# Sinks as a column of the softmax, and fewer small operations in cross-attention, in a two-layer encoder kernel

## The chip, the cores and the metric

The kernel runs on one core of one Trainium2 chip. What counts is the device time of one execution in microseconds (us). Engine names are those of the profile: PE is the matrix engine (TensorE), PEld its weight loads, DVE the vector engine (VectorE), ACT the scalar engine (ScalarE), POOL GpSimd, SP the engine that issues most transfers.

## What is computed

Two layers of a bidirectional encoder on 1024 tokens of width 1024, float32. Each layer has a token mixer and a gated feed-forward part with a short convolution; the mixer of layer 0 is windowed attention, that of layer 1 a gated linear recurrence (HGRN2). Beside either mixer run four heads of cross-attention into 256 memory tokens. The parts that matter here, cut:

```python
def window_gqa_sink(q, k, v, sink):          # 16 heads in 4 groups, blocks of 128 queries, band of 384 keys
    s = einsum('bnqhgd,bnkhd->bnhgqk', qb, kb) * (d ** -0.5)          # d = 64, factor 0.125
    s = where(valid, s, -inf)
    m = maximum(max(s, axis=-1), sk)                                  # sk: one sink per head
    p = exp(s - m)
    p = p / (sum(p, axis=-1) + exp(sk - m))
    o = einsum('bnhgqk,bnkhd->bnqhgd', p, vb)

def memory_cross_attn(xq, mem_kv):           # 4 heads of 128
    s = einsum('bthd,bmhd->bhtm', q, k) * (128 ** -0.5)
    o = einsum('bhtm,bmhd->bthd', softmax(s), v)

# layer: h = h + rmsnorm(mixer(rmsnorm(h))); h = h + rmsnorm(conv_ffn(rmsnorm(h)))
```

## The kernel before

A float32 product is made of three matmuls: each operand is split into a rounded part and a remainder, and `mm3` adds high times high, high times low and low times high. `split(h, l, src)` makes the two parts with a cast on ACT (L88) and a subtraction on DVE (L89); `wunit` does the same for weights that come from memory (L78 on ACT, L79 on DVE or, for some of the first mixer's weights, on POOL). So nearly every matmul has an ACT and a DVE instruction ahead of it.

The program is written as one sequence; a planner puts the instructions of each engine into an order with a simulated timeline of its own, by priority and by when operands are ready there. Each engine then runs its list in order, and waits only where data or a buffer is missing. `tc.high_priority` and `tc.issue_after` steer single instructions. Tiles come from pools with a fixed number of buffers per tag; a new tile waits until the last reader of the buffer is done.

The order of the work: `start` (0 to some 60 us) prepares the memory tokens and the first input; `window` (to about 500 us) is the first mixer; then its output projection and the first feed-forward part (`ffn`, to about 1200 us); `hgrn` (to about 1950 us) is the second mixer with its output projection behind it; then the second feed-forward part.

In `window`, `proj(g)` makes queries, keys and values of one group of four heads, with rotary factors multiplied on DVE (L297, L298) and added on POOL (L299, L300), transposed by PE (L322). `attend(g, qkv, blocks)` goes over eight blocks of 128 queries; projection of the next group, attention of this one and cross-attention units are interleaved by the planner. A block of `attend` is a chain:

- per head j of four: two matmuls give the scores in one of two PSUM banks (tag `ps`, L374 and L375), and one DVE scan (L377, a custom operation with an accumulator read behind it) adds the mask, writes the sum to the score buffer `sm` and keeps the running maximum, begun at eight times the sink (`sk8`), in `mx`;
- three small instructions make the negated maximum `nm` (L380) and the sink's exponential `es` (L381 on DVE, L382 on ACT);
- four exponentials on ACT (L384) with their row sums in `su`; DVE adds `es` (L389) and takes the reciprocal `rd` (L390);
- four multiplies by `rd`, two on ACT (L393) and two on DVE (L395), then per 128 keys four transposes on PE (L400), a split of the result (L88, L89), and two matmuls with the values (L403, L404); L406 and L407 add the halves of the result.

The score buffer has three copies and is shared (tag `sm`) with the probabilities of cross-attention (`xp`) in this mixer. GpSimd's list in this mixer holds the rotary additions, some weight remainders (L79), the roots of `rooted`, and the issues of memory-to-memory transfers that add feed-forward weights (`second_sums`, L144 and L146).

`cross_unit(l, h, b, ...)` does one head and 512 queries of cross-attention, eight units in each layer: projection (24 matmuls), split of the queries, scores of four times 128 queries, a maximum over two of them at a time (L219), its scaling (L221 in layer 0, where a factor per token `xsc` comes in; L223 in layer 1), an exponential each (L226), one reciprocal (L228), four multiplies (L230), transposes (L235), split, product with the values.

Of the kernel before, what the change touches and what calls it, by code (L numbers as in the profile page):

```python
# [8 lines left out]
F32 = mybir.dt.float32  # L9
# [3 lines left out]
AF = mybir.ActivationFunctionType  # L13
ALU = mybir.AluOpType
AX = mybir.AxisListType
# [3 lines left out]
P = 128  # L19
T = 1024  # L20
D = 1024
NT = T // P
# [4 lines left out]
XSCALE = float(np.float32(128.0 ** -0.5))  # L27
# [22 lines left out]
def build(tc, A, out):  # L50
    nc = tc.nc
    act, dve, pool, pe = nc.scalar, nc.vector, nc.gpsimd, nc.tensor
    bc = lambda ap, shape: ap.to_broadcast(shape)
# [28 lines left out]
    def mm3(o, ah, al, bh, bl, first, last):  # L82
        pe.matmul(o, ah, bh, start=first, stop=False)  # L83
        pe.matmul(o, ah, bl, start=False, stop=False)  # L84
        return pe.matmul(o, al, bh, start=False, stop=last)  # L85

    def split(h, l, src):
        act.copy(h, src)  # L88
        dve.tensor_tensor(l, src, h.bitcast(F32), op=ALU.subtract)  # L89
# [110 lines left out]
    def cross_unit(l, h, b, head, wp, tags, w0, pair, dead=False):  # L200

        wh, wl, kvh, kvl = head
        ps = tags["pj"][2].tile([P, 512], F32, tag=tags["pj"][0], bufs=tags["pj"][1], name="pj")
        for k in range(KT):
            c = slice(k * P, (k + 1) * P)
            m = slice(b * 512, (b + 1) * 512)
            mm3(ps, wh[:, c], wl[:, c], uh[:, k, m], ul[:, k, m], k == 0, k == KT - 1)
        xh, xl = pair("x", b)
        with tc.high_priority(AHEAD):
            split(xh, xl, ps)  # L210
        p = wp.tile([P, 4, 256], F32, tag="sm", bufs=tags["sm"], name="xp")
        st = {x: wp.tile([P, 4], F32, tag=x, name=x) for x in ("nm", "su", "rd")}
        for i in range(2):
            s = tags["ps"][2].tile([P, 2, 256], F32, tag=tags["ps"][0], bufs=tags["ps"][1], name="ps")
            for j in range(2):
                m = slice((2 * i + j) * P, (2 * i + j + 1) * P)
                mm3(s[:, j, :], xh[:, m], xl[:, m], kvh[:, 0, :], kvl[:, 0, :], True, True)
            e = slice(2 * i, 2 * i + 2)
            dve.reduce_max(st["nm"][:, e], s, axis=AX.X)  # L219
            if l == 0:  # L220
                dve.tensor_tensor(st["nm"][:, e], st["nm"][:, e], xsc[:, 1, 4 * b + 2 * i:4 * b + 2 * i + 2], op=ALU.mult)  # L221
            else:
                dve.tensor_scalar_mul(st["nm"][:, e], st["nm"][:, e], -XSCALE)  # L223
            for j in range(2):
                q = 2 * i + j
                act.activation(p[:, q, :], s[:, j, :], AF.Exp, bias=st["nm"][:, q:q + 1],  # L226
                               scale=xsc[:, 0, 4 * b + q:4 * b + q + 1] if l == 0 else XSCALE, accum_out=st["su"][:, q:q + 1])
        dve.reciprocal(st["rd"], st["su"])  # L228
        for q in range(4):
            dve.tensor_scalar_mul(p[:, q, :], p[:, q, :], st["rd"][:, q:q + 1])  # L230
        po = tags["po"][b]()
        for m in range(2):
            tp = tags["pt"][2].tile([P, 4, P], F32, tag=tags["pt"][0], bufs=tags["pt"][1], name="pt")
            for q in range(4):
                pe.transpose(tp[:, q, :], p[:, q, m * P:(m + 1) * P], ident)  # L235
            ph, pl = pair("p", m)
            split(ph, pl, tp.rearrange("p a b -> p (a b)"))
            hd = slice(m * P, (m + 1) * P)
            mm3(po, kvh[:, 1, hd], kvl[:, 1, hd], ph, pl, m == 0, m == 1)
        ot = p[:, :2, :].rearrange("p a b -> p (a b)") if dead else w0.tile([P, 512], F32, tag=tags.get("xo", "xo"), bufs=1, name="xo")  # L240
        act.copy(ot, po)
        act.dma_start(oT[l][8 + h, :, b * 512:(b + 1) * 512], ot)


    def window():
        ea = tc.alloc_tile_pool(name="attn0", bufs=1, reuse_waits="tile")
        ap_ = tc.alloc_tile_pool(name="attn", bufs=2, side="right", reuse_waits="tile")
        psq = tc.alloc_tile_pool(name="aps0", bufs=1, space=PSUM, reuse_waits="tile")
        psp = tc.alloc_tile_pool(name="aps", bufs=1, space=PSUM, side="right", reuse_waits="tile")
        for x in ("mx", "nm"):  # L250
            ap_.tile([P, 4], F32, tag=x, name=x)
        wmask = ap_.tile([P, 384], F32, bufs=1, name="wmask")
        sk = ap_.tile([P, 16], F32, bufs=1, name="sk")
        sk8 = ap_.tile([P, 16], F32, bufs=1, name="sk8")
        ap_.tile([64, 4, 256], F32, tag="o", bufs=2, name="o")
        for x, n in (("kh", 1), ("kl", 1), ("v", 1), ("qs", 8), ("sm", 3), ("ph", 2), ("pl", 2)):
            if x == "v":
                ap_.tile([P, NT, P], F32R, tag=x, bufs=n, name=x)
            elif x == "sm":
                ap_.tile([P, 4, 384], F32, tag=x, bufs=n, name=x)  # L260
            else:
                ap_.tile([P, 512 if n > 1 else T], F32R, tag=x, bufs=n, name=x)
        nc.sync.dma_start(wmask, A["wmask"])
        nc.sync.dma_start(sk, A["a_sink"].to_broadcast([P, 16]))
        c4 = lambda ap: ap.rearrange("p (h a c) -> p h a c", a=2, c=32)

        tags = {"pj": ("pj", 2, psq), "ps": ("ps", 2, psp), "pt": ("pt", 2, psp), "po": [lambda: psp.tile([P, 512], F32, tag="po", bufs=1, name="po")] * 2, "sm": 3}
# [80 lines left out]
        marks, moved = {}, []  # L348

        def split_moved():  # L350
            ts_ = moved.pop()
            oh, ol = uh[:, 6:8, ts_], ul[:, 6:8, ts_]
            act.copy(oh, ol.bitcast(F32))
            dve.tensor_tensor(ol, ol.bitcast(F32), oh.bitcast(F32), op=ALU.subtract)

        def attend(g, qkv, blocks=range(NT)):
            qs, kh, kl, v = qkv
            for b in range(2):
                for nn in range(4):
                    n = 4 * b + nn  # L360
# [5 lines left out]
                    lo, hi = max(n - 1, 0), min(n + 2, NT)  # L366
                    w = (hi - lo) * P
                    mo = (lo - (n - 1)) * P
                    sm = ap_.tile([P, 4, 384], F32, tag="sm", bufs=3, name="sm")
                    st = {x: ap_.tile([P, 4], F32, tag=x, name=x) for x in ("mx", "nm", "es", "su", "rd")}  # L370
                    for j in range(4):
                        s = psp.tile([P, 384], F32, tag="ps", bufs=2, name="ps")
                        m = slice(nn * P, (nn + 1) * P)
                        pe.matmul(s[:, :w], qs[j][b][:, m], kh[:, lo * P:hi * P], start=True, stop=False)  # L374
                        pe.matmul(s[:, :w], qs[j][b][:, m], kl[:, lo * P:hi * P], start=False, stop=True)  # L375
                        hd = 4 * g + j
                        dve.tensor_tensor_reduce(out=sm[:, j, :w], in0=s[:, :w], in1=wmask[:, mo:mo + w],  # L377
                                                 scale=1.0, scalar=sk8[:, hd:hd + 1], op0=ALU.add, op1=ALU.max,
                                                 accum_out=st["mx"][:, j:j + 1])
                    dve.tensor_scalar_mul(st["nm"], st["mx"], -0.125)  # L380
                    dve.tensor_tensor(st["es"], sk[:, 4 * g:4 * g + 4], st["nm"], op=ALU.add)  # L381
                    act.activation(st["es"], st["es"], AF.Exp)  # L382
                    for j in range(4):
                        marks[g, n] = act.activation(sm[:, j, :w], sm[:, j, :w], AF.Exp, bias=st["nm"][:, j:j + 1],  # L384
                                                     scale=0.125, accum_out=st["su"][:, j:j + 1])
                    if moved and n % 2 == 0:
                        with tc.issue_after(marks[g, n].ins):
                            split_moved()
                    dve.tensor_tensor(st["su"], st["su"], st["es"], op=ALU.add)  # L389
                    dve.reciprocal(st["rd"], st["su"])  # L390
                    for j in range(4):
                        if j < 2:
# [4 lines left out]
                    for c in range(hi - lo):  # L397
# [3 lines left out]
                        ph, pl = pair("p", c)  # L401
# [24 lines left out]
                        xhead[0] = cross_head(0, xh_, ea, None if xh_ else marks[0, 3])  # L426
                    cross_unit(0, xh_, xb_, xhead[0], ap_, tags, ea, pair)

        dve.tensor_scalar_mul(sk8, sk, 8.0)
        cur = proj(0)  # L430
        for g in range(3):
            attend(g, cur, range(0 if g else 3, NT))
# [948 lines left out]

    x0 = tc.alloc_tile_pool(name="x0", bufs=1, side="right", reuse_waits="tile")
    rs0 = x0.tile([P, NT], F32, name="rs0")
    xsc = x0.tile([P, 2, NT], F32, name="xsc")
    xss = x0.tile([P, NT], F32, name="xss")
    tables = tc.alloc_tile_pool(name="tables", bufs=1, reuse_waits="tile")
    cos = tables.tile([P, NT, 32], F32, name="cos")
# [2 lines left out]
    def rooted(t, *turns):  # L1390
        c = slice(t, t + 1)
        dve.tensor_scalar(xss[:, c], xss[:, c], 1.0 / D, EPS, op0=ALU.mult, op1=ALU.add)
        pool.tensor_tensor(rs0[:, c], xss[:, c], nhalf[:, c], op=ALU.pow)
        for x in turns:
            dve.tensor_scalar_mul(x, x, rs0[:, c])
        dve.tensor_scalar_mul(xsc[:, 0, c], rs0[:, c], XSCALE)
        dve.tensor_scalar_mul(xsc[:, 1, c], rs0[:, c], -XSCALE)

    def start():
        pss = tc.alloc_tile_pool(name="mps", bufs=1, space=PSUM, reuse_waits="tile")  # L1400
# [186 lines left out]
```

## Time and profile before

| | us |
|---|---|
| median of 3 runs | 2660.64 |
| the runs | 2657.53 to 2662.38 |
| the profiled execution | 2656.7 |
| its span, first to last instruction | 2654.6 |

| engine | busy us of the span | instructions |
|---|---|---|
| PE | 2598.7 (98%) | 14420 |
| DVE | 1818.1 (68%) | 3043 |
| ACT | 1377.3 (52%) | 2503 |
| POOL | 472.4 (18%) | 520 |

The granted TensorE clock was 0.999 over the span. A matmul with 512 columns stands in the profile with 0.39 us, but the next one begins 0.23 us after it: they are pipelined and their ends are modelled, so a busy PE is not a PE at its peak. In a row of a group the numbers are the busy time of all, the mean of one in ns, and the idle time of the engine just before them with what ended it. In a row of waits they are the total, how often, and the longest, in us.

### The profile page before, as it was taken

How to read it: one execution, taken by the hardware profiler on the slowest of the kernel's cores; microseconds unless marked ns; L12 is line 12 of the kernel's file. 1: busy time of each engine (PE TensorE's matmuls, PEld its weight loads, DVE VectorE, ACT ScalarE, POOL GpSimd, SP SyncE). 2: the span in 40 equal slices, each digit the busy share in tenths (PEclk: the TensorE clock that was granted, in tenths of full speed). 3: DMA queues.
4: the chain of work that ended last, by engine and by line, in shares of the span. 5: the costliest groups of instructions: out<-in, count | busy, mean ns of one | idle time of the engine just before them, and what ended most of it. 6: DMA issues, size and time to landing. Idle time of an engine off the chain costs nothing. (4 is left out here: it accounts for less than half of the span.)

```text
span 2654.6 us, 39112 instructions
## 1 busy us (share of the span) xinstructions
PE 2598.7 (98%) x14420; PEld 2184.3 (82%) x14420; DVE 1818.1 (68%) x3043; ACT 1377.3 (52%) x2503; POOL 472.4 (18%) x520
## 2 busy tenths in 40 slices
PE   8999999999999999999999999999999999999998
PEld 7888887788888888887888888888887788888887
DVE  6688886577655565478688686886757755656447
ACT  6467676545444445454465554555534444445443
POOL 0421010211111100031224131231311111110013
PEclk9999999999999999999999999999999999999999
DMA  9782232367777857674235351103437778785656
GB/s 354 246 174 58 74 91 81 107 190 192 200 202 193 209 154 257 191 251 150 84 112 150 81 128 53 52 25 100 141 105 197 194 191 211 197 202 168 224 192 238
DMA packets 195728, 425.93 MB, mean 160 GB/s; under 512 B 20048, under 2 KB 56272, under 8 KB 189904
## 3 DMA queue, kind: packets, MB, share of 16 engines
q1 hardware_dynamic: 161552, 324.06, 37.7%
q0 software_dynamic: 24544, 90.19, 16.3%
q10 hardware_dynamic: 9440, 9.19, 1.1%
q8 instruction: 113, 1.85, 0.3%
q14 instruction: 79, 0.65, 0.1%
HBM read 330.04 MB, written 116.39 MB: 168 GB/s over the span
## 5 line engine op out<-in xcount | busy, mean ns | idle before, releaser
L89 DVE TENSOR_TENSOR wl<-st,wh 128x1024 fp32r<-128x1024 f32 (+1 forms) x238 | 262.7, 1110 | 317.0 <-ACT wh L88 289.0
L88 ACT CAST wh<-st 128x1024 fp32r<-128x1024 f32 (+1 forms) x238 | 222.4, 936 | 287.2 <-PE X L592 189.7
L83 PE MATMUL pj<-uh,wh 128*128 128x512 f32 x512 | 202.8, 396 | 3.8 <-DVE q L1143 1.8
L592 PE MATMUL X<-wl,wh 128*128 128x512 f32 x528 | 204.6, 389 | 0.0
L592 PE MATMUL X<-wh,wl 128*128 128x512 f32 x528 | 204.5, 389 | 0.0
L85 PE MATMUL pj<-uh,wl 128*128 128x512 f32 x512 | 202.0, 395 | 0.0
L84 PE MATMUL pj<-ul,wh 128*128 128x512 f32 x512 | 201.9, 394 | 0.1
L592 PE MATMUL X<-wh 128*128 128x512 f32 x528 | 198.7, 390 | 1.0 <-ACT c L1006 1.0
L83 PE MATMUL pj<-wh,uh 128*128 128x384 f32 (+1 forms) x512 | 189.3, 371 | 4.7 <-DVE gs L1129 2.5
L85 PE MATMUL pj<-wh,ul 128*128 128x384 f32 (+1 forms) x512 | 187.2, 366 | 0.0
L84 PE MATMUL pj<-wl,uh 128*128 128x384 f32 (+1 forms) x512 | 186.6, 364 | 0.0
L79 DVE TENSOR_TENSOR wl<-st,wh 128x1024 fp32r<-128x1024 f32 (+1 forms) x91 | 115.2, 1272 | 29.3 <-ACT wh L78 28.6
L592 PE MATMUL V<-uh,wh 128*128 128x512 f32 x336 | 130.7, 389 | 0.0
L592 PE MATMUL V<-ul,wh 128*128 128x512 f32 x336 | 130.7, 389 | 0.0
L592 PE MATMUL V<-uh,wl 128*128 128x512 f32 x336 | 130.7, 389 | 0.0
L78 ACT CAST wh<-st 128x1024 fp32r<-128x1024 f32 (+1 forms) x97 | 97.8, 1014 | 46.1 <-PE pj L84 24.2
L592 PEld LDWEIGHTS X<-wh 128*128 128x128 f32 x528 | 99.1, 188 | 22.0 <-ACT c L1006 1.4
L83 PEld LDWEIGHTS pj<-uh,wh 128*128 128x128 f32 x512 | 96.3, 188 | 24.0 <-DVE q L1143 2.6
L592 PEld LDWEIGHTS X<-wl,wh 128*128 128x128 f32 x528 | 99.1, 188 | 20.5
L592 PEld LDWEIGHTS X<-wh,wl 128*128 128x128 f32 x528 | 99.1, 188 | 20.4
L975 POOL TENSOR_TENSOR c<-c,g 128x512 f32<-128x512 f32 x24 | 43.4, 1824 | 388.5 <-DMA st<-hid 159.7
L84 PEld LDWEIGHTS pj<-ul,wh 128*128 128x128 f32 x512 | 96.3, 188 | 18.6 <-DVE ul L89 0.4
(413 smaller groups left out, 7221.8 us busy)
## 6 DMA issues: line engine op xcount, KB each, us to landing
st<-hid SPq DMA_DIRECT2D x154, 256.0 KB, 3.0
st<-in_ffw_dram SPq DMA_DIRECT2D x108, 256.0 KB, 3.4
w2s<-in_ffw_dram POOLq DMA_DIRECT2D x24, 1024.0 KB, 8.7
st<-in_ffw_dram SPq DMA_DIRECT2D x46, 512.0 KB, 4.4
hid<-tt SPq DMA_DIRECT2D x88, 256.0 KB, 4.7
st<-w2s SPq DMA_DIRECT2D x88, 256.0 KB, 3.0
sx<-in_ffw_dram SPq DMA_DIRECT2D x84, 256.0 KB, 3.9
sy<-in_ffw_dram SPq DMA_DIRECT2D x42, 512.0 KB, 7.1
```

What stands on the lines that cost most here:

```text
L78: act.copy(h[:, :n], raw)
L79: (eng or dve).tensor_tensor(l[:, :n], raw, h[:, :n].bitcast(F32), op=ALU.subtract)
L83: pe.matmul(o, ah, bh, start=first, stop=False)
L84: pe.matmul(o, ah, bl, start=False, stop=False)
L85: return pe.matmul(o, al, bh, start=False, stop=last)
L88: act.copy(h, src)
L89: dve.tensor_tensor(l, src, h.bitcast(F32), op=ALU.subtract)
L592: last = pe.matmul(o, x, y, start=new, stop=e, skip_group_check=not first)
L975: pool.tensor_tensor(y[q][:, t, :], y[q][:, t, :], g3[:, c], op=ALU.mult)
```

## The change

In the windowed attention the sinks become column 385 (or 257 at the two ends of the sequence) of the score buffer: POOL copies the four negated sinks of a group there (`sk` is negated once, `sk8` goes). The scan writes the masked scores multiplied by -0.125 and keeps their minimum, begun at the negated sink, which is the negated maximum `nm` itself. The exponentials run over one more column with the factor -1, so their row sum holds the sink's term. `mx`, `es` and the three small DVE operations and the small ACT operation go. Rows of the buffer are 385 long, and so are those that cross-attention of layer 0 uses 256 of; the buffer is placed behind the others, and two pads are added.

In cross-attention the maximum comes out negated. In layer 0 one column of scales is left. In layer 1 the factor goes into the split of the queries (a scaled copy on ACT, a scaled subtraction on DVE), so that the scaling of the maximum goes. In both layers one DVE operation with a broadcast reciprocal takes the place of the four multiplies.

```diff
         with tc.high_priority(AHEAD):
-            split(xh, xl, ps)
-        p = wp.tile([P, 4, 256], F32, tag="sm", bufs=tags["sm"], name="xp")
+            if l == 0:
+                split(xh, xl, ps)
+            else:
+                act.activation(xh, ps, AF.Copy, scale=XSCALE)
+                dve.scalar_tensor_tensor(xl, ps, XSCALE, xh.bitcast(F32), op0=ALU.mult, op1=ALU.subtract)
+        p = wp.tile([P, 4, 385 if l == 0 else 256], F32, tag="sm", bufs=tags["sm"], name="xp")[:, :, :256]
...
-            dve.reduce_max(st["nm"][:, e], s, axis=AX.X)
+            dve.reduce_max(st["nm"][:, e], s, axis=AX.X, negate=True)
             if l == 0:
-                dve.tensor_tensor(st["nm"][:, e], st["nm"][:, e], xsc[:, 1, 4 * b + 2 * i:4 * b + 2 * i + 2], op=ALU.mult)
-            else:
-                dve.tensor_scalar_mul(st["nm"][:, e], st["nm"][:, e], -XSCALE)
+                dve.tensor_tensor(st["nm"][:, e], st["nm"][:, e], xsc[:, 4 * b + 2 * i:4 * b + 2 * i + 2], op=ALU.mult)
...
-                               scale=xsc[:, 0, 4 * b + q:4 * b + q + 1] if l == 0 else XSCALE, accum_out=st["su"][:, q:q + 1])
+                               scale=xsc[:, 4 * b + q:4 * b + q + 1] if l == 0 else 1.0, accum_out=st["su"][:, q:q + 1])
         dve.reciprocal(st["rd"], st["su"])
-        for q in range(4):
-            dve.tensor_scalar_mul(p[:, q, :], p[:, q, :], st["rd"][:, q:q + 1])
+        dve.tensor_tensor(p, p, bc(st["rd"].unsqueeze(2), [P, 4, 256]), op=ALU.mult)
...
-        for x in ("mx", "nm"):
+        for x in ("nm", "su"):
             ap_.tile([P, 4], F32, tag=x, name=x)
...
-        sk8 = ap_.tile([P, 16], F32, bufs=1, name="sk8")
...
-        for x, n in (("kh", 1), ("kl", 1), ("v", 1), ("qs", 8), ("sm", 3), ("ph", 2), ("pl", 2)):
+        for x, n in (("kh", 1), ("kl", 1), ("v", 1), ("qs", 8), ("ph", 2), ("pl", 2)):
...
-            elif x == "sm":
-                ap_.tile([P, 4, 384], F32, tag=x, bufs=n, name=x)
...
+        ap_.tile([P, 8], F32, bufs=1, name="pad")
...
-                    sm = ap_.tile([P, 4, 384], F32, tag="sm", bufs=3, name="sm")
-                    st = {x: ap_.tile([P, 4], F32, tag=x, name=x) for x in ("mx", "nm", "es", "su", "rd")}
+                    sm = ap_.tile([P, 4, 385], F32, tag="sm", bufs=3, name="sm")
+                    st = {x: ap_.tile([P, 4], F32, tag=x, name=x) for x in ("nm", "su", "rd")}
+                    pool.tensor_copy(sm[:, :, w:w + 1], sk[:, 4 * g:4 * g + 4].unsqueeze(2))
...
-                                                 scale=1.0, scalar=sk8[:, hd:hd + 1], op0=ALU.add, op1=ALU.max,
-                                                 accum_out=st["mx"][:, j:j + 1])
-                    dve.tensor_scalar_mul(st["nm"], st["mx"], -0.125)
-                    dve.tensor_tensor(st["es"], sk[:, 4 * g:4 * g + 4], st["nm"], op=ALU.add)
-                    act.activation(st["es"], st["es"], AF.Exp)
+                                                 scale=-0.125, scalar=sk[:, hd:hd + 1], op0=ALU.add, op1=ALU.min,
+                                                 accum_out=st["nm"][:, j:j + 1])
                     for j in range(4):
-                        marks[g, n] = act.activation(sm[:, j, :w], sm[:, j, :w], AF.Exp, bias=st["nm"][:, j:j + 1],
-                                                     scale=0.125, accum_out=st["su"][:, j:j + 1])
+                        marks[g, n] = act.activation(sm[:, j, :w + 1], sm[:, j, :w + 1], AF.Exp, bias=st["nm"][:, j:j + 1],
+                                                     scale=-1.0, accum_out=st["su"][:, j:j + 1])
...
-                    dve.tensor_tensor(st["su"], st["su"], st["es"], op=ALU.add)
                     dve.reciprocal(st["rd"], st["su"])
...
-        dve.tensor_scalar_mul(sk8, sk, 8.0)
+        dve.tensor_scalar_mul(sk, sk, -1.0)
...
-    xsc = x0.tile([P, 2, NT], F32, name="xsc")
+    xsc = x0.tile([P, NT], F32, name="xsc")
+    x0.tile([P, NT], F32, name="pad")
...
-        dve.tensor_scalar_mul(xsc[:, 0, c], rs0[:, c], XSCALE)
-        dve.tensor_scalar_mul(xsc[:, 1, c], rs0[:, c], -XSCALE)
+        dve.tensor_scalar_mul(xsc[:, c], rs0[:, c], XSCALE)
```

## The prediction

> **What bounds the kernel now.** I read the page's busy times first, then the busy times by stage, then who waited for whom in the first mixer.
>
> ```profile
> span 2654.6 us, 39112 instructions
> PE 2598.7 (98%) x14420; PEld 2184.3 (82%) x14420; DVE 1818.1 (68%) x3043; ACT 1377.3 (52%) x2503; POOL 472.4 (18%) x520
> ```
>
> ```profile
> core 0: us, PE busy (x) PEld busy (x) DVE busy (x) ACT busy (x) POOL busy (x), PEclk, DMA share, GB/s
> 60.00:500.00 440.00, 415.62 (x2308) 364.02 (x2307) 333.34 (x886) 286.54 (x707) 71.90 (x101) 1.00 0.42 116
> 500.00:1200.00 700.00, 698.07 (x3125) 577.86 (x3124) 442.47 (x501) 338.89 (x470) 110.44 (x107) 1.00 0.71 204
> 1200.00:1900.00 700.00, 689.58 (x5367) 580.89 (x5366) 545.16 (x1066) 370.84 (x792) 182.89 (x195) 1.00 0.32 92
> ```
>
> TensorE bounds the whole, at full granted clock. The change removes no matmul, so it can win only what TensorE idles: 440 - 415.6 = 24.4 us in the first mixer (60 to 500 us) and 700 - 689.6 = 10.4 us in the second one (1200 to 1900); the stretch between has 1.9 us. So some 35 us are at stake, most of them in the first mixer, where VectorE is busy 333.3 / 440 = 76%.
>
> ```profile
> PEld ps L374 <- DVE mx L377: 15.6, 26, 1.7
> PE ps L374 <- DVE mx L377: 8.9, 14, 1.4
> PEld po L404 <- DVE pl L89: 6.1, 8, 1.6
> PE po L404 <- DVE pl L89: 3.3, 5, 1.2
> PEld po L403 <- DVE o L407: 2.5, 5, 1.1
> PEld pj L83 <- DVE xl L89: 2.4, 3, 1.1
> PE pj L83 <- DVE xl L89: 1.6, 3, 1.0
> PE po L403 <- DVE o L407: 1.3, 2, 0.9
> ACT sm L384 <- DVE nm L380: 15.4, 11, 3.4
> DVE sm L377 <- PE pt L400: 10.5, 6, 5.7
> DVE su L389 <- ACT es L382: 5.1, 4, 2.0
> ```
>
> Columns: total us, times, longest. Four places where TensorE waits for VectorE carry its idling. Counted as idle matmul time they are 8.9 + 3.3 + 1.3 + 1.6 = 15.1 us; counted at the weight loads, 15.6 + 6.1 + 2.5 + 2.4 = 26.6 us. I take the second: modelled ends of pipelined matmuls cover the start of a wait, which is why 26 waits shrink to 14. The largest is the score matmul (L374), which wants a bank that the masked scan (L377) has yet to empty.
>
> **The change, part by part.** Durations are from the profiled execution (2656.7 us, span 2654.6); it lies 3.9 us under the median of the runs, 2660.6. The differences below are made on the first and set off from the second.
>
> ```profile
> L380 DVE TENSOR_SCALAR nm<-mx 128x4 f32<-128x4 f32 x32 | 9.0, 281 | 0.3
> L389 DVE TENSOR_TENSOR su<-su,es 128x4 f32<-128x4 f32 x32 | 5.8, 182 | 12.6 <-ACT sm L384 7.3 <-ACT es L382 5.1
> L381 DVE TENSOR_TENSOR es<-sk,nm 128x4 f32<-128x4 f32 x32 | 5.6, 174 | 0.4
> L230 DVE TENSOR_SCALAR xp<-xp,rd 128x256 f32<-128x256 f32 x32 | 14.6, 519 | 0.4
> L79 DVE TENSOR_TENSOR xwl<-st,xwh 128x1024 fp32r<-128x1024 f32 x2 | 2.4, 1220 | 0.0
> L395 DVE TENSOR_SCALAR sm<-sm,rd 128x384 f32<-128x384 f32 x48 | 19.0, 437 | 0.4
> L377 DVE CUSTOM_DVE_ANT_0 sm<-ps,wmask,sk 128x384 f32<-128x384 f32 x96 | 57.0, 611 | 28.7 <-PE ps L375 20.3 <-PE pt L400 8.1
> L1397 DVE TENSOR_SCALAR xsc<-rs 128x1 f32<-128x1 f32 x7 | 1.0, 144 | 0.0
> ```
>
> ```profile
> 92.63 3.95 DVE L380 TENSOR_SCALAR nm<-mx 128x4 f32<-128x4 f32 x1
> ```
>
> *1. VectorE's small work, first mixer.* Each of the 32 blocks loses three 128x4 operations: 9.0 + 5.6 + 5.8 = 20.4 us. One of them is a single L380 of 3.95 us, beside two weight subtractions on GpSimd; whatever VectorE issues next would meet the same, so 3.8 of it stays: 16.6 us go. The second column of scales goes: 1.0 us.
>
> *2. The four normalizing multiplies of cross-attention become one.* Undisturbed, four overlap and end after 1.14 us; the one that replaces them is as long as L79's 128x1024 form, 1.22 us.
>
> ```profile
> 273.24 5.00 DVE L230 TENSOR_SCALAR xp<-xp,rd 128x256 f32<-128x256 f32 x4
> 1321.63 1.14 DVE L230 TENSOR_SCALAR xp<-xp,rd 128x256 f32<-128x256 f32 x4
> ```
>
> ```profile
> 274.35 3.74 POOL L79 TENSOR_TENSOR wl<-st,wh 128x768 fp32r<-128x768 f32 x2
> ```
>
> So the merge by itself costs 0.08 us a unit. It may still win in layer 0, where the 8 units take 14.6 us against 8 x 1.22 = 9.8: there two of four multiplies stretched to the length of GpSimd's operations beside them (5.00 against 3.74), and one instruction can be caught fewer times than four. Bounds 0 and -4.8; I take half, -2.4. [...]
>
> VectorE then loses 16.6 + 1.0 + 2.4 = 20.0 of 333.3 us: its share falls from 0.758 to 0.712. If waiting behind a queue goes as share / (1 - share), from 3.13 to 2.47, it falls by 21%: 0.21 x 26.6 = 5.6 us of TensorE's waits (3.2 by the lower count). Bounds: 20.0 x 26.6/440 = 1.2 if only what VectorE does during a wait counts; all 26.6 if the removed work were what kept every scan late. I take -5.6.
>
> *3. The chain of a block.* From the last scan to the normalized probabilities go the negation (0.16), the sink's exponential and the add (0.16):
>
> ```profile
> L382 ACT ACTIVATE es<-es 128x4 f32<-128x4 f32 x32 | 6.3, 197 | 0.1
> L384 ACT ACTIVATE sm<-sm,nm 128x384 f32<-128x384 f32 x96 | 58.0, 607 | 10.1 <-DVE nm L380 9.9
> L384 ACT ACTIVATE sm<-sm,nm 128x256 f32<-128x256 f32 x32 | 16.0, 501 | 5.5 <-DVE nm L380 5.5
> ```
>
> That is 0.52 us a block, 16.6 us in all; ScalarE also gets 6.3 us back and pays 128 x (607 - 501)/128 ns = 0.1 us for the added columns. It is covered by the matmuls of the projection and of neighbouring blocks nearly everywhere; TensorE idles 24.4/440 = 6% of the time, which gives 0.9 us; at most the 5.1 us that VectorE waits for the sink's exponential. I take -2.0. The scan with a factor and a minimum, the negated maximum (L219) and the exponentials with another constant stay the same instructions on the same tiles: 0, though no row shows the new forms. Next latest is the scan itself: ScalarE's 15.4 us of waiting for L380 turn into waiting for L377.
>
> *4. GpSimd's new copy of the sinks*, 32 times. The trace has no such copy in this mixer; the nearest are a 128x64 addition there and the 128x4 strided copy of the second mixer (minimum/median/maximum):
>
> ```profile
> L300 POOL TENSOR_TENSOR rq<-t,t 128x64 f32<-128x64 f32 x32 | 10.6, 332 | 0.0
> L1259 POOL COPY dec<-EP x32: 177/584/3792, 1251.4 to 1890.7; 128x4 f32<-128x4 f32 x32
> ```
>
> It has the shape of the second, so 0.58 us. It waits for a score buffer whose last transposes are done, three blocks back, and stands in GpSimd's queue before rotary additions (L299, L300), weight subtractions and the issues of memory-to-memory transfers; TensorE waits for the rotary additions. Six times (10.5 us) the scan itself waited for that buffer; if it waits for the copy too, 6 x 0.58 = 3.5 us. Bounds 0 and 32 x 0.58 = 18.7. GpSimd is busy 72 of 440 us, so mostly the copy is early: +1.0.
>
> *5. Odd rows of 385.* The multiplies (L395) still take even widths. If they lost their speed they would be as long as a scan: 0.17 us x 64 = 11 us of VectorE, a quarter of it on TensorE. No row shows it: 0, with +3 in the range.
>
> *6. Second mixer.*
>
> ```profile
> L223 DVE TENSOR_SCALAR nm<-nm 128x2 f32<-128x2 f32 x16 | 2.4, 161 | 0.1
> L89 DVE TENSOR_TENSOR xl<-pj,xh 128x512 fp32r<-128x512 f32 x8 | 5.5, 686 | 10.2 <-ACT xh L88 10.2
> L1319 DVE SCALAR_TENSOR_TENSOR ul<-pt,bng,uh 128x512 fp32r<-128x512 f32 x1 | 0.7, 743 | 0.0
> ACT xp L226 <- DVE nm L223: 16.8, 5, 3.9
> ```
>
> Sixteen negations go (2.4 us); eight subtractions become scaled ones (8 x 0.06 = 0.5) and eight merges add 0.6: 1.3 of 545 us, nothing by itself. The exponentials that waited for L223 start 0.16 us sooner: 5 x 0.16 = 0.8 at most, -0.5 taken. The scaled copy on ScalarE has the form of the unscaled one: 0. No DMA is added or moved. The score buffers lie elsewhere in the memory and two pads are new: addresses alone, priced with the planner below.
>
> Sum: -5.6 - 2.0 + 1.0 - 0.5 = -7.1 us: 2649.6 for an execution like the profiled one, 2653.5 for the median. The planner lays all queues anew for other durations; this can give or take anywhere in the two mixers, and I can only bound it by the 35 us of idling.
>
> **Rivals.**
>
> *A, hidden.* All that goes was slack of VectorE (107 us idle in the mixer): -1.2 from part 2, and the copy gives it back: 2660. For it: the scan's own 0.61 us a head, unchanged, sets the pace in a burst of four heads against two banks. Against: VectorE waits only 28.7 us before scans, so mostly other work keeps them late.
>
> *B, slower: the copy gates the scan.* Copy and scan write one tile; if the scan is held until the copy lands and the copy is as late as the buffer, every block pays 0.58 us: 18.7 - 8.1 = +10.6, 2671. It turns slower from 8.1/0.58 = 14 blocks of 32. For it: the 3.8 us maximum of L1259, copies that were held up. Against: only six blocks are short of buffers. [...]
>
> *C, more.* The bursts are tightly coupled, and half of the 26.6 us goes with 2 of the chain: -15, 2645.
>
> **How the numbers follow.** My forecast (-3 to -12) has 0.45, A 0.17, B 0.18, C 0.20. What counts as no change is 0.2%, 5.3 us. Of the 0.45, 0.32 lies beyond it: faster 0.32 + 0.20 = 0.52; same 0.13 + 0.17 = 0.30; slower 0.18. The range runs from 2640, past C, to 2668, short of B's full price; outside remain 2 in 10. The likeliest case alone spans 2648 to 2658.
>
> **What would show it.** After: L374's waits at the weight loads near 12 us instead of 15.6, TensorE busy over 420 of the mixer's 440 us or the mixer shorter, VectorE near 313 us there, the copy at 0.2 to 0.6 us with no scan or exponential waiting for GpSimd, and the merged multiply at 1.22 us. Wrong would be: scans that wait for GpSimd (B); waits at L374 unchanged (A); multiplies at L395 of 0.6 us (part 5); or a difference that sits after 500 us, which no step above accounts for.

## The result, and the profile after

| | before | after |
|---|---|---|
| median us | 2658.45 (2657.53 to 2662.38, 6 runs) | 2643.78 (2642.75 to 2646.71, 6 runs) |
| profiled execution, its span | 2656.7, 2654.6 | 2646.5, 2644.4 |

The ratio of after to before is 0.9944, with a 95% interval of 0.9931 to 0.9957: the change is faster by 14.7 us, beyond the 0.2% that counts, and inside the range of the prediction. It is twice the forecast of -7.1 us, though, and lands on rival C (2645). So the question of the experiments is where the other half comes from, and whether the first half came from where the prediction said.

The page's busy times and the busy times by stage, after:

```profile
span 2644.4 us, 38978 instructions
PE 2598.7 (98%) x14420; PEld 2187.7 (83%) x14420; DVE 1807.8 (68%) x2875; ACT 1379.0 (52%) x2471; POOL 486.7 (18%) x552
```

```profile
60.00:500.00 440.00, 425.01 (x2352) 374.51 (x2351) 319.51 (x761) 290.73 (x680) 85.05 (x133) 0.99 0.43 119
500.00:1200.00 700.00, 697.60 (x3123) 577.49 (x3122) 450.54 (x515) 340.31 (x473) 113.69 (x110) 1.00 0.72 205
1200.00:1900.00 700.00, 690.96 (x5388) 583.59 (x5387) 546.77 (x1027) 373.09 (x798) 182.60 (x193) 1.00 0.32 93
```

TensorE is busy for the same 2598.7 us; the span shrank by idle time alone. In the stretch of the first mixer its idling fell from 24.4 to 15.0 us, elsewhere by little. Laid against each other matmul by matmul (the start of the nth one after, less that of the nth one before), the two profiled executions are 10.0 us apart at the 2700th matmul, at the end of the first mixer, gain 1.5 us more in the second, and end 10.2 apart. The profiled execution of after is a long one of its six, and that of before is shorter than all of its six; hence 10 here and 14.7 in the medians.

Who waited for whom, after. The order of TensorE's instructions is another, and lines have moved: L396 is the transposes (L400 before), L399 and L400 the products with the values (L403, L404), L381 the exponentials (L384), L391 the multiplies on DVE (L395), L231 the merged multiply.

```profile
PEld ps L374 <- DVE nm L377: 4.5, 11, 0.7
PEld po L400 <- DVE pl L89: 4.5, 10, 1.3
PEld po L399 <- ACT ph L88: 4.3, 6, 1.4
ACT sm L381 <- DVE nm L377: 38.4, 34, 4.6
DVE sm L377 <- PE ps L375: 24.5, 22, 4.5
```

The last of these rows, for the kernel before:

```profile
DVE sm L377 <- PE ps L375: 25.7, 23, 3.3
```

The wait of the score matmul's weight load for the scan fell from 15.6 to 4.5 us, much further than the forecast 12. Scans wait for the score matmuls as long as before (24.5 against 25.7 us). Their wait for a score buffer, 10.5 us in six waits before, is 0.7 us in two; the row of L377 below, for the 384 columns alone, has 0.2 of it.

The exponentials now wait for the scans, 38.4 us in 34 waits against 15.4 in 11 for L380 before. It is more than the "late next" that the prediction named, because the change does more than take instructions away: L380 read the maxima of all four heads, so no exponential could start before the fourth scan was done; now the exponential of a head needs that head's own column of `nm`. One block before (its last scan, its first and its last exponential), then one after (its second and third scan and exponential):

```profile
144.28 0.60 DVE L377 CUSTOM_DVE_ANT_0 sm<-ps,wmask,sk 128x384 f32<-128x384 f32 x1
146.40 0.62 ACT L384 ACTIVATE sm<-sm,nm 128x384 f32<-128x384 f32 x1 [1.61 <-DVE nm L380]
148.22 0.60 ACT L384 ACTIVATE sm<-sm,nm 128x384 f32<-128x384 f32 x1
```

```profile
134.65 0.62 DVE L377 CUSTOM_DVE_ANT_0 sm<-ps,wmask,sk 128x384 f32<-128x384 f32 x1 [1.25 <-PE ps L375]
135.31 0.62 ACT L381 ACTIVATE sm<-sm,nm 128x385 f32<-128x385 f32 x1 [1.48 <-DVE nm L377]
136.47 0.62 DVE L377 CUSTOM_DVE_ANT_0 sm<-ps,wmask,sk 128x384 f32<-128x384 f32 x1 [1.20 <-PE ps L375]
137.13 0.62 ACT L381 ACTIVATE sm<-sm,nm 128x385 f32<-128x385 f32 x1 [0.60 <-DVE nm L377]
```

In the trace before, no block of the 32 has an exponential ahead of its fourth scan; after, all 32 have. From the end of the last scan to the end of the reciprocal it takes 5.66 us before and 1.81 after (medians of the 32 blocks). These two figures, how many blocks start early and how long the rest takes, are given for the experiments too.

```profile
L377 DVE CUSTOM_DVE_ANT_0 sm<-ps,wmask,sk 128x384 f32<-128x384 f32 x96 | 56.8, 610 | 19.1 <-PE ps L375 18.6 <-PE pt L396 0.2
L391 DVE TENSOR_SCALAR sm<-sm,rd 128x384 f32<-128x384 f32 x48 | 19.2, 442 | 0.4
L231 DVE TENSOR_TENSOR xp<-xp,rd x16: 1217/1225/1461, 159.7 to 1824.2; 128x1024 f32<-128x1024 f32 x16
L370 POOL COPY sm<-sk x32: 179/190/1080, 68.5 to 456.0; 128x4 f32<-128x4 f32 x32
```

The rows of single operations came as taken or better (the last two are minimum/median/maximum in ns): the new scan costs the old one's 0.61 us, odd rows leave the multiplies at 442 ns (437 before), the copy takes 0.19 us.

### The profile page after: what moved, and what is told of

Same layout as the page of the kernel before. It is cut to its first block, busy times and chain, and to the rows that moved or that the text cites. A ratio compares the mean times of both kernels' runs of the same rounds, so it can differ in the third digit from the quotient of the medians.

```text
span 2644.4 us, 38978 instructions
## 1 busy us (share of the span) xinstructions
PE 2598.7 (98%) x14420; PEld 2187.7 (83%) x14420; DVE 1807.8 (68%) x2875; ACT 1379.0 (52%) x2471; POOL 486.7 (18%) x552
## 5 line engine op out<-in xcount | busy, mean ns | idle before, releaser
L79 DVE TENSOR_TENSOR wl<-st,wh 128x1024 fp32r<-128x1024 f32 (+1 forms) x91 | 118.3, 1305 | 33.9 <-ACT wh L78 33.3
L83 PEld LDWEIGHTS pj<-uh,wh 128*128 128x128 f32 x512 | 96.3, 188 | 22.8 <-DVE q L1139 2.9
```

The source lines that it names most:

```text
L79: (eng or dve).tensor_tensor(l[:, :n], raw, h[:, :n].bitcast(F32), op=ALU.subtract)
```

## The experiments

Three theories stood at the start. T: less VectorE work and a shorter chain of a block, as forecast, only with larger sizes. L: the planner's new order of the queues is a lucky one, and the work removed matters little. X: the cross-attention part carries what the forecast lacks. (In the recorded expectations T is theory W and L is rival O; theory P there is the work and the order together.) All ratios are to the kernel before.

**One part at a time.** `attn_only` has the changes of `attend` and its buffers, with cross-attention as before; `cross_only` the reverse.

> Only the windowed attention is changed (sinks as a column, scan with the factor and the minimum, the three small VectorE operations and the small ScalarE one gone, rows of 385); cross-attention is as before in both layers. Theory W (the gain is the work that left VectorE and the chain of a block): nearly all of the 14.7 us, ratio 0.994 to 0.996, and TensorE's waits at L374 for the scan near 5 us at the weight loads, against 15.6. Rival O (the gain is another lay of the queues that the planner made, with the removed work as its mere occasion): any ratio from 0.993 to 1.003, since the order differs from both kernels' in the first mixer.

> Only cross-attention is changed, in both layers; the windowed attention is as before. Theory W: little, ratio 0.998 to 1.000: 1 to 2 us from VectorE's share in the first mixer, 0.5 to 1.5 us in the second. Rival O: any ratio from 0.995 to 1.003. If the two parts add up to the whole (0.9944), W is the simpler account.

Measured: attention alone 0.9953 (0.9941 to 0.9966), cross-attention alone 0.9995 (0.9986 to 1.0004). Their product, 0.9948, is the whole change within its interval. X falls; most of the gain is made in the windowed attention. The figure of cross-attention hides something, though: in its run ScalarE waits for a load of keys and values that comes late, as theory D below has it, and TensorE loses 3.7 us at that place.

```profile
216.43 0.62 ACT L196 CAST kvh<-kvl 128x512 fp32r<-128x512 f32 x1 [5.36 <-DMA kvl<-kvd]
```

So 0.9995 leaves room for some 4 us of gain without that wait. No run shows them.

**Work and order apart.** A planner lays 39,000 instructions anew when a duration changes, so an edit of work is an edit of order as well. These two kernels hold TensorE's order by edges that bind the order of issue alone, called behind the build of the program (cut to the call and what it does):

```diff
+    in_order(tc)   # for consecutive a, b of a list of PE's instructions in both mixers:
+                   #   tc.add_manual_dep(pe[b], pe[a].name, NoSync)
```

The first does the new work in TensorE's old order, the second the old work in TensorE's new order; the other queues were laid by the planner around it.

> The whole change, but TensorE issues its instructions in exactly the order that it has in the kernel before (edges of issue order alone, no waits); the queues of VectorE, ScalarE and GpSimd are laid anew around it. Theory W: most of the gain stays, ratio 0.994 to 0.997. Rival O: the gain goes with the order, ratio 0.998 to 1.002.

> The kernel before in all its work, but TensorE issues its instructions in exactly the order that it has in the changed kernel. Theory W: no gain, ratio 0.999 to 1.006 (an order made for shorter chains may cost). Rival O: the gain comes with the order, ratio 0.993 to 0.997.

Measured: 1.0043 (1.0030 to 1.0057) and 1.0080 (1.0067 to 1.0093). Both are slower than before, and outside the ranges of both theories. Stage rows and waits, the first kernel and then the second:

```profile
60.00:500.00 440.00, 411.15 (x2248) 362.79 (x2247) 311.69 (x749) 282.65 (x667) 83.27 (x133) 0.97 0.42 115
PEld ps L374 <- DVE nm L377: 18.4, 25, 1.7
```

```profile
60.00:500.00 440.00, 398.10 (x2202) 353.23 (x2202) 322.29 (x870) 282.93 (x694) 74.36 (x101) 0.97 0.41 113
PEld pt L400 <- ACT sm L393: 28.0, 16, 8.4
```

With the old order TensorE asks for scores as closely behind the scans as before, and waits even longer (18.4 us) in spite of the lighter VectorE. With the new order and the old work, it asks for the transposes of a block before its longer chain is done (28.0 us, up to 8.4 at once): the new order counts on the short chain. So neither the work nor TensorE's order gives the gain by itself. The exponentials start early in 31 of the first kernel's 32 blocks (1.74 us from the last scan to the reciprocal) and in none of the second's (4.79), so early exponentials aren't enough either. Much of both losses is clock, though: the mean granted clock, averaged over the runs, is 0.995 and 0.993, against 0.998 of the kernel before on the same chip, which is about 8 of the 11.4 us that the first loses and 12 of the 21.3 of the second (a lower share of 2660 us). The first has the late load as well (8.6 us to landing, TensorE loses 3.5 us there). Without both it would be near no change. In all other kernels here this mean is 0.997 to 0.999.

Those two mix an imposed order with new ones. `removed_nothing_relaid` is the attention's change with all five queues exactly as before, the removed instructions left out and only GpSimd's copies placed freely. `copy_added` is the opposite piece: the kernel before with rows of 385 and the copies, nothing removed.

> The windowed attention is changed as in the run of that part alone, but the instructions that both kernels have stand on all five queues in exactly the order of the kernel before; only GpSimd's copies of the sinks are placed by the planner. So the work is gone and nothing is laid anew. Theory W (the removed VectorE work and the shorter chain pay by themselves): ratio 0.995 to 0.998. Theory P (the work lets the planner place TensorE's instructions for a shorter chain, and the gain comes from order and chain together): little here, 0.998 to 1.000, with TensorE's waits for the scan at L374 near the 15.6 us of before.

> The kernel before with rows of 385 in the score buffer and GpSimd's copy of the sinks into each block's buffer added; nobody reads that column, all the rest of the work stays, and TensorE's order is the one of before. By the prediction's terms 4 and 5: +1 us (bounds 0 and 18.7 for the copy, 0 to 11 of VectorE for the odd rows): ratio 1.000 to 1.002. If rival B held: 1.007.

Measured: 1.0000 (0.9991 to 1.0009) and 1.0027 (1.0018 to 1.0036). In the first, VectorE has lost its work (321.2 us in the mixer's stretch) and nothing came of it. The old list of ScalarE also keeps the exponentials where they were: 5 of 32 blocks start them early, and it is 5.40 us from the last scan to the reciprocal. Its waits:

```profile
60.00:500.00 440.00, 415.73 (x2303) 364.18 (x2302) 321.15 (x789) 283.58 (x675) 80.62 (x133) 1.00 0.42 116
PEld ps L373 <- DVE nm L376: 16.0, 27, 1.8
```

In the second, 1.0027 lies above the expected 1.000 to 1.002, and nearly all of TensorE's delay against the kernel before, 6.1 us, arises at one place, between 215 and 222 us; the first loses 4.0 us there too. The load of a head's keys and values for cross-attention lands late. Below are, for the kernel before and then for `removed_nothing_relaid`, the issues and the first use (start, duration, engine, operation; in brackets the idle time and what ended it), and the transfers issued from 200 to 225 us (KB, us from issue to landing):

```profile
208.29 0.86 POOL L144 DMA_DIRECT2D w2s<-w2s  x1
208.79 0.33 SPq L194 DMA_DIRECT2D kvl<-kvd  x1
212.57 0.62 ACT L196 CAST kvh<-kvl 128x512 fp32r<-128x512 f32 x1 [1.56 <-DMA kvl<-kvd]
w2s<-w2s POOLq DMA_DIRECT2D x1, 1024.0 KB, 9.7
kvl<-kvd SPq DMA_DIRECT2D x1, 256.0 KB, 3.8
```

```profile
207.51 0.86 POOL L144 DMA_DIRECT2D w2s<-w2s  x1
208.18 0.33 SPq L194 DMA_DIRECT2D kvl<-kvd  x1
216.53 0.62 ACT L196 CAST kvh<-kvl 128x512 fp32r<-128x512 f32 x1 [7.28 <-DMA kvl<-kvd]
w2s<-w2s POOLq DMA_DIRECT2D x1, 1024.0 KB, 8.8
kvl<-kvd SPq DMA_DIRECT2D x1, 256.0 KB, 8.3
```

In `removed_nothing_relaid` the load of 256 KB lands with the 1 MB memory-to-memory transfer that GpSimd issued 0.67 us ahead of it (208.18 + 8.3 against 207.51 + 8.8 us). That made theory D: in the old queues the removed work does pay, and the late load takes it away. The planner's new lay has the load at 192.0 us, clear of that transfer, and it lands in 2.9 us.

**D tested.** `early_load` is `removed_nothing_relaid` with a second buffer for that tile and SP's queue laid freely, so that the second head's load is issued at 65 us:

```diff
-        kvl = wp.tile([P, 2, 256], F32R, tag="kvl", bufs=1, name="kvl")
+        kvl = wp.tile([P, 2, 256], F32R, tag="kvl", bufs=1 if l else 2, name="kvl")
```

> The run in which the work is gone and nothing is laid anew, with a second buffer for the raw keys and values of the memory tokens in the first mixer, so that the load for the second head of cross-attention is issued some 140 us sooner; the queues of TensorE, VectorE, ScalarE and GpSimd stay exactly as in the kernel before. There that load was issued 0.7 us behind the start of the issue of a memory-to-memory transfer of 1 MB (208.2 against 207.5 us) and landed after 8.3 us, with ScalarE idle for 7.3; in the kernel before, 0.5 us behind it, it landed after 3.7. Theory D (a share of what the unchanged queues showed is this collision): TensorE's delay against the kernel before at 220 us goes from +3 to -1 us, ratio 0.9980 to 0.9990 instead of 1.0000. Against D: 0.9995 to 1.0005.

Measured: 0.9979 (0.9971 to 0.9988), 5.6 us less than `removed_nothing_relaid` and a hair more gain than D's range. D is right: the loss between 215 and 222 us is gone. Up to 1.6 us of the gain can be the wait that the kernel before has at the same place (its row above), which the early load removes too; the early load in the kernel before wasn't tried. TensorE's wait for the scans is as long as ever (14.8 us), so what the work pays here doesn't come from there.

**Load or chain.** Both of these start from the change. `load_back` gives VectorE three small operations per block back, off the chain; `chain_back` lengthens the chain by two GpSimd copies and leaves VectorE as light as it is; as its first copy reads the minima of all four heads, it also makes every exponential wait for the fourth scan again. Both are laid anew by the planner.

```diff
+                    idle = ap_.tile([P, 4], F32, tag="idle", name="idle")          # load_back
+                    for _ in range(3):
+                        dve.tensor_tensor(idle, sk[:, 4 * g:4 * g + 4], st["nm"], op=ALU.add)
...
+                    pool.tensor_copy(st["n2"], st["nm"])     # chain_back: n2 is the exponentials' bias
+                    pool.tensor_copy(st["s2"], st["su"])     # chain_back: s2 goes into the reciprocal
```

> The whole change, with three 128x4 VectorE operations put back in each of the 32 blocks, behind the scan and off the chain: they read the negated maximum and write a tile that nobody reads. Load (VectorE's share sets the waits, the prediction's largest term): most of the 5.6 us and more of the gain goes, ratio 0.997 to 1.000. Chain (the latency of a block sets them): the gain stays, 0.993 to 0.996.

> The whole change, with the chain of a block made longer again without VectorE: GpSimd copies the negated maximum before the exponentials and the row sums before the reciprocal, 2 x 0.19 us and the hand-overs, in each of the 32 blocks. Load: the gain stays, 0.993 to 0.996. Chain: it goes, 0.998 to 1.003. Either is blurred if GpSimd's queue holds the copies up, which its waits would show.

Measured: 0.9941 (0.9928 to 0.9953) and 0.9968 (0.9955 to 0.9980). `load_back`, then `chain_back`:

```profile
60.00:500.00 440.00, 426.82 (x2363) 375.27 (x2362) 332.95 (x861) 297.27 (x694) 90.86 (x138) 1.00 0.44 123
PEld ps L374 <- DVE nm L377: 7.6, 18, 1.0
```

```profile
60.00:500.00 440.00, 422.18 (x2351) 373.14 (x2350) 319.54 (x763) 290.16 (x691) 104.97 (x201) 1.00 0.44 123
PEld ps L374 <- DVE nm L377: 11.2, 16, 2.5
ACT sm L382 <- POOL n L380: 18.3, 12, 4.7
DVE rd L388 <- POOL s L387: 22.8, 18, 3.2
kvl<-kvd SPq DMA_DIRECT2D x1, 256.0 KB, 8.5
```

VectorE is as busy again as before the change (332.95 against 333.34 us) and the kernel is as fast as the change: its load is worth nothing that shows, and by the two intervals at most some 4 us. Its exponentials start early in all 32 blocks. With the longer chain 0.0024 are given back, 6.4 of the 14.7 us, with VectorE at its lighter 319.5; that lies between the ranges of the two theories. No exponential starts early there, and it is 4.12 us from the last scan to the reciprocal. So this chain grew by far more than two copies: the fourth scan holds all exponentials, and ScalarE and VectorE wait for GpSimd's copies, 18.3 us in 12 waits and 22.8 in 18, up to 4.7 us at once, as the last rows of waits show. Nor need all of the 6.4 be the chain: the planner put the load beside the 1 MB transfer again, and the mean clock of these runs is 0.9966 against 0.9982 of the change's, some 4 us. Whether the longer waits bring that lower clock isn't shown.

**The copy, and another lay.** `copy_on_vector` makes the copies of the sinks on VectorE instead of GpSimd. The last two take the four heads of a block in the order 3, 2, 1, 0 (`for j in range(3, -1, -1)` at the scores), before and after: the same work in another lay.

> The whole change with the copies of the sinks on VectorE instead of GpSimd. Three such operations a block behind the scan cost nothing; this one stands ahead of it, 0.16 us, and waits for the same buffer as the scan. If GpSimd's copy still costs in the changed kernel what it cost in the old queues (0.0027): ratio 0.992. If the new order had hidden it: 0.994 to 0.995, the same as the change.

> The kernel before with the four heads of a block scored in the order 3, 2, 1, 0: the same instructions and the same work, but the planner lays the first mixer anew (2199 of its TensorE positions differ). Theory P (shorter chains give better orders): the ratio stays near 1, 0.998 to 1.002. Rival L (any new lay is a draw, and the change drew a good one): anywhere from 0.994 to 1.006.

> The changed kernel with the heads scored in the order 3, 2, 1, 0: the same work, another lay. Theory P: 0.993 to 0.996, as the change. Rival L: anywhere from 0.994 to 1.006, and its distance to the reversed kernel before has no sign.

Measured: 0.9952 (0.9939 to 0.9964), 0.9982 (0.9973 to 0.9991) and 0.9935 (0.9921 to 0.9948). Taking the copies off GpSimd doesn't gain anything, so there they are hidden. Reversed heads help the kernel before by 4.8 us: its own lay was not its best, and one lay more or less is worth that much. Against that better lay the change with reversed heads still gains 0.9935 / 0.9982, or 12.5 us. Its 2639.7 us is the fastest median of all, but its interval overlaps the change's. Its stage row and the one of `before_heads_reversed`:

```profile
60.00:500.00 440.00, 426.72 (x2378) 378.63 (x2377) 327.52 (x764) 296.64 (x692) 88.69 (x137) 1.00 0.45 124
```

```profile
60.00:500.00 440.00, 420.63 (x2317) 369.26 (x2316) 326.84 (x886) 287.91 (x707) 72.98 (x101) 0.99 0.43 117
```

L in its plain form falls with these: the five freely laid kernels with the short chain and no extra copies in it (the change, `attn_only`, `load_back`, `copy_on_vector`, `after_heads_reversed`) lie between 0.9935 and 0.9953, the four with the old chain (before, `cross_only`, `copy_added`, `before_heads_reversed`) between 0.9982 and 1.0027. In the five, 31 or 32 of the 32 blocks start their exponentials early and 1.6 to 2.0 us pass from the last scan to the reciprocal; in the four, none does and it is 5.2 to 5.8 us. What remains of L is that the order has to follow the chain: with the old queues, in which the part behind the last scan hardly shortens (5.40 us against 5.66), the change gives 5.6 us at best, with queues laid for it 14.7.

## Why the prediction was right or wrong

Right in place and sign: the gain is idle time of TensorE in the first mixer, cross-attention gives little, and nothing after 500 us carries the difference. Low by half in size. By its steps:

1. *VectorE's small work, -5.6 by share/(1 - share).* This is the term that failed. VectorE's load went to 319.5 us, near the forecast 313 (the stretch to 500 us holds some 10 us more of the program than before), but `load_back` puts it back to 333 and loses nothing: in the lay of the change the term measures 0, with 4 us as the most that the intervals allow. In the old queues the removed work pays 4.0 to 5.6 us (`early_load`), and whether as load or as a slightly shorter chain isn't shown. TensorE's waits did fall by more than forecast, 15.6 to 4.5 us at L374, but with the order: 18.4 with the same light VectorE in the old TensorE order, 7.6 with the heavy one in a new lay, and 7.7 in `before_heads_reversed`, which has all of the old work. So what keeps a scan late is, as far as these runs show, where it stands in the sequence and not a queue in front of it, and a queue formula doesn't price that. The episode of 3.95 us beside GpSimd did pass to another instruction, an L391 pair of the changed kernel, beside two of GpSimd's weight subtractions (3.65 us from 92.79 us on):

```profile
92.95 3.90 DVE L391 TENSOR_SCALAR sm<-sm,rd 128x256 f32<-128x256 f32 x2
```

2. *The merged multiply, -2.4 of VectorE's work.* It measures 1.225 us in the median, as the row of L79 said; the 8 units of layer 0 come to 10.0 us against 14.6, near the bound of -4.8. In time it gives nothing measurable, 0.9995 for all of cross-attention, with the late load in that run as a reservation.

3. *The chain, -2.0.* Mis-sized. It was counted as the 0.52 us of the removed instructions and priced by the time that TensorE idled. What it had wrong is the wait: with L380 went the wait of the first three exponentials for the fourth scan, so that the chain behind the last scan is 3.85 us shorter (5.66 against 1.81), if the queues are laid for it. `chain_back`, which brings this wait back, gives 6.4 us back, with GpSimd's delays, a late load and some clock in it. A shorter chain lets the planner place a block's transposes earlier and frees a score buffer sooner (10.5 us of scans' waits became 0.7, and 11.3 in `chain_back`), and that isn't in the share of idle time. No run brings back the wait for the fourth scan alone, so its own worth stays open.

4. *The copy, +1.0.* In the change's lay 0 (`copy_on_vector`: 0.9952 against 0.9944); in the old queues the copies stand between rotary additions, and `copy_added` loses 7.2 us, nearly all by the late load. No scan or exponential waits for GpSimd after, so rival B is wrong: the copy takes 0.19 us, not 0.58, and comes early. That it might move a DMA issue, and so delay a load, was not seen.

5. *Odd rows, 0.* Right: 442 against 437 ns.

6. *Second mixer, -0.5.* The trace has -1.5 us there, `cross_only` can't tell it from 0. The scaled subtraction costs the unscaled one's 686 ns, not 0.06 us more:

```profile
L214 DVE SCALAR_TENSOR_TENSOR xl<-pj,xh 128x512 fp32r<-128x512 f32 x8 | 5.5, 686 | 6.8 <-ACT xh L213 6.8
```

7. *The planner's new order, bounded by 35 us and taken as 0.* This carried the difference between the 5.6 us that the work gives in the old queues and the 14.7 measured: some 9 us. The sum of -7.1 came near the 5.6 of the held queues by luck: by a term that measures zero in the new lay and one that is too small.

Rival A was right on VectorE's load and wrong on the result; C was right on the size, but put most of it on VectorE's work.

What stays open: how the 9 us divide between the load that the new lay happens to issue earlier, TensorE's better order, the exponentials' early start, and what a longer chain costs in clock. `removed_nothing_relaid` against `early_load` prices the collision at 0.0021, 5.6 us, but the kernel before bears at most 1.6 of it. And the 12.5 us between the two kernels with reversed heads hold no collision at all, as the load is clear of the transfer in both (2.7 and 3.7 us to landing). So the early load can't be much of the gain. The new lay with its load moved back beside the transfer wasn't tried.

## What to carry to other kernels

In a coupled pipeline, price a removed instruction by whether it stands on the chain between two uses of the bound engine, not by the load of an engine that isn't the bound; adding the same load back off the chain is the test (here 0.9941 with the load back against 0.9944, and 0.9968 with a longer chain, a late load and some clock in it). Ask also for how many operands it waits: one small instruction that reads the results of four heads holds everything behind it until the fourth is done (here none of 32 blocks had an early exponential with it, all 32 without). Where a planner orders the queues, a change of work is a change of order: hold the order to see the work, let it go to see the sum, and run a second lay of both kernels before you believe either. Look at what each DMA issue is moved next to: the same load landed in 2.9 us or in 8.3 here.

## What the hardware showed that was not expected

*A small load that lands with a large one.* Loads of 256 KB issued by SP 0.6 to 0.9 us after GpSimd's issue of a 1 MB memory-to-memory transfer began took 7.6 to 8.9 us to land in six kernels; in the seven in which the second head's load was clear of it (issued at 191.7 to 204.3 us), that load took 2.7 to 3.7 us. The kernel before issued its load 0.5 us after, and it landed in 3.8 us. The packets in the traces tell the two cases apart. The transfer (queue q0) is 128 packets of 8192 bytes, the load (q1) 128 packets of 2048. Below are packets, MB and busy share of each queue, in `removed_nothing_relaid` from 210.4 to 213.4 us and in the kernel before from 209.5 to 211.05 us:

```profile
q0 software_dynamic: 66, 0.54, 87.0%
q1 hardware_dynamic: 68, 0.14, 17.6%
```

```profile
q1 hardware_dynamic: 73, 0.15, 75.1%
```

In the first the transfer's packets begin at 209.1 us and the load's at 210.4; from there the two queues begin about as many packets, 66 and 68 in the 3 us, and both end at 216.0: the load, with as many packets as the transfer and a quarter of its bytes, ends with it. In the second the load's packets begin first, at 209.8 us, and 73 of them have begun before the transfer's first, at 211.1. What decides which begins first isn't shown.

*The clock fell behind a wait of 1.9 us, and not behind 1.7 us of idling in the kernel before.* The third figure from the right is the granted clock. Three stretches of `after_pe_order_before`, with TensorE's longest wait there (it ends at 311.1 us), then one of the kernel before:

```profile
308.00:316.00 8.00, 6.12 (x31) 5.34 (x30) 6.48 (x19) 6.96 (x18) 0.00 (x0) 0.79 0.00 1
312.50:316.00 3.50, 3.50 (x16) 3.26 (x15) 2.37 (x7) 2.51 (x8) 0.00 (x0) 0.51 0.00 0
316.00:324.00 8.00, 6.93 (x36) 5.67 (x35) 4.67 (x8) 4.41 (x13) 0.00 (x0) 1.00 0.15 33
PE pt L396 <- DVE pl L89: 1.9, 1, 1.9
```

```profile
116.00:124.00 8.00, 6.29 (x37) 5.39 (x36) 5.42 (x12) 3.75 (x10) 2.22 (x4) 1.00 0.59 210
```

By the 0.79 of the first row, a dip of this kind costs an estimated 8 x 0.21 = 1.7 us. In the first mixer eight of this kernel's stretches of 8 us lie under 0.99, two of the change's, none of the kernel before, though one of it idles nearly as much (1.7 of 8 us against 1.9). If the dip belongs to the wait ahead of it, which only their order in time suggests, an idle microsecond of TensorE can cost nearly two (1.9 us of wait and 1.7 of dip), and the idle time alone doesn't say which. In the 3.5 us of the second row the clock was 0.51, and no matmul of this kernel's first mixer waited longer than 1.9 us. What brings the clock down isn't shown.
